# A two-layer diffusion backbone on one core: the order of every engine written out by the program, and the modulation spread over more stages

## The chip, the core and the metric

The kernel runs on one core of a Trainium2 chip. A core has five engines that run side by side and meet through semaphores: TensorE (matmuls; PE in the profile, PEld its weight loads), VectorE (DVE), ScalarE (ACT), GpSimd (POOL) and SyncE (SP), the last two used here mostly to issue DMAs. Each engine works off its own queue in order. The metric is the device time of one launch in microseconds (us).

## The reference, cut to what matters

Two layers over 256 latent tokens of width 1024, with 256 context tokens that only the first layer reads. Each layer is FFN half step, token mixing, FFN half step. Each sub-layer is wrapped in two RMS norms and a modulation that is computed from a conditioning vector:

```python
def pre(x, m, k, g):                       # shift and scale
    return rms_norm(x, g) * (1 + m[:, 3*k+1, None]) + m[:, 3*k, None]
def post(y, m, k, g):                      # gate
    return m[:, 3*k+2, None] * rms_norm(y, g)
def swiglu(h, w_gu, w_down):
    gt, up = jnp.split(h @ w_gu, 2, axis=-1)
    return (jax.nn.silu(gt) * up) @ w_down
m_lat = ada_mod(c, w_mod[i], b_mod[i])     # silu(c) @ w + b: nine vectors of 1024 per layer
x = x + 0.5 * post(swiglu(pre(x, m, 0, g[0]), ff1...), m, 0, g[1])
x = x + post(mixer(pre(x, m, 1, g[2])), m, 1, g[3])
x = x + 0.5 * post(swiglu(pre(x, m, 2, g[4]), ff2...), m, 2, g[5])
```

The first layer's mixer joins a depthwise convolution of 31 taps with a group norm (512 channels) and attention of 8 heads over a window with a bias plus all context keys. The second layer's mixer is a gated convolution of 3 taps. All inputs are float32.

## The kernel before, in words

**Weights.** All weight matrices lie in one flow of chunks of 16 tiles (128x128 each), in the order of use. `load` (L187) brings half a chunk (512 KB) on SP's queue; `piece` (L193) splits four tiles into a rounded part (`nc.scalar.copy`, L202) and a remainder (`nc.vector.tensor_sub`, L203). Every product is three matmuls (rounded x rounded, rounded x remainder, remainder x rounded): `mm3` (L213 to L217) with the weights stationary and 256 or 512 tokens moving, `rows3` (L286 to L291) with 128 tokens stationary and 512 output columns moving.

**Stages.** ff1_0 (latent and context, 512 tokens), ev_in, attention and convolution, ev_out, ff2_0, ff1_1, od_in, od_out, ff2_1. An FFN computes `gate_up` (silu on ScalarE, product on VectorE, split on both; L330 to L334) for each of 22 groups of 128 columns, then the down matmuls. In ff1_0 this goes in five parts of 4, 4, 4, 5 and 5 groups; the first three groups of part one are accumulated together (`grp`) while the inputs are being normalised, and after each part's groups its down matmuls run for four blocks of 128 tokens (L537 to L539). In the later FFNs the first three groups are computed token-major (`head`, L317), and `Out` (L295) runs the down matmuls for two token blocks: all but the last 6 rows of tiles for both blocks, then that tail (`TAIL`) for the first block and for the second.

**Norm steps.** `residual` (L246) squares the block, multiplies by the gate row, takes the power -1/2 on POOL (L240), updates x (L258) and repeats square and power for the next norm. `turn` (L265) scales the rows, transposes them on TensorE (L274), applies scale and shift per channel (L279) and splits (L283, L284).

**Modulation.** 128 tiles of `wmodb` (512 KB each) come on POOL's queue into four slots; `mod_dot` (L129) reduces one with the conditioning vector on VectorE, the first 24 tiles twice (latent and context). `bg(n)` does the next n dots: 4 after each group of ff1_0 and 2 after each down block (`BG0`), one per group in ff2_0 (`BG1`), the rest at ff2_0's end. `gate_row` (L169) writes the gate vector to DRAM and reads it back onto all partitions as a row, both on POOL's queue.

**Order.** The program emits instructions as its loops run; a planner then orders each engine's queue by its own estimates and priorities. `high_priority(offset=AHEAD)` moves the norm steps up. The convolution's taps (L599) are handed out between attention steps by fixed counts (`CONV_AT`); `scores` and `weigh` do one head pair and token block at a time.

Of the kernel before, what the change touches and what calls it, by code (L numbers as in the profile page):

```python
# [47 lines left out]
AHEAD = 300  # L48
MOD_PE = (0, 1, 2, 4, 6)
PARTS0 = (4, 4, 4, 5, 5)  # L50
BG0 = (4, 2)
BG1 = 1
CONV_AT = (2, 4, 6, 10, 8, 8)
CONV_ORDER = ((0, 0), (0, 1), (1, 0), (0, 2), (1, 1), (0, 3), (1, 2), (1, 3))
EV_ORDER = (6, 4, 5, 0, 1, 2, 3, 7)
EV_TAIL = 4
RING = 12
EXTRA = ("X2", "X3", "Y2", "Y3")
# [4 lines left out]
def hybrid_kernel(ctx: ExitStack, tc: tile.TileContext, xT, ctxT, xtok, crow, smalls, wmoda, wmodb, wflow, bias,  # L63
# [5 lines left out]
    wraw = ctx.enter_context(tc.tile_pool(name="wraw", bufs=5))  # L69
    whi = ctx.enter_context(tc.tile_pool(name="whi", bufs=RING))  # L70
    wlo = ctx.enter_context(tc.tile_pool(name="wlo", bufs=RING))
    mraw_p = ctx.enter_context(tc.tile_pool(name="mraw", bufs=4))
# [3 lines left out]
    ps_mm = ctx.enter_context(tc.tile_pool(name="ps_mm", bufs=6, space=bass.MemoryType.PSUM))  # L76
    ps_bc = ctx.enter_context(tc.tile_pool(name="ps_bc", bufs=2, space=bass.MemoryType.PSUM))

    def bank(pool, name):
        return pool.tile([P, 512], F32, name=name)  # L80
# [32 lines left out]
    for n in range(4):  # L113
        ps = bank(ps_mm, "mm")
        nc.tensor.matmul(ps, lhsT=ident[0:4, n:n + 1].to_broadcast([4, P]), rhs=crow_t, start=True, stop=True)
        nc.scalar.activation(cbf[:, n * 512:(n + 1) * 512], ps, AF.Silu)
# [11 lines left out]
    def mod_dot(row, l, v, ch, j):  # L128
        nc.vector.scalar_tensor_tensor(junk, row, 1.0, cb[:, v, :], op0=ALU.mult, op1=ALU.mult,  # L129
                                       accum_out=mraw[:, l, v, ch, j:j + 1])  # L130

    def mod_jobs():
        order = [(0, 2, (0, 1)), (0, 3, (0, 1)), (0, 4, (0, 1))]
        order += [(0, ch, (0,)) for ch in (5, 6, 7, 8)] + [(1, ch, (0,)) for ch in range(9)]
        n = 0
        for l, ch, conds in order:
            for j in range(KD):
                cur = mraw_p.tile([P, D], F32, name="mr", tag="mr")
                nc.gpsimd.dma_start(out=cur, in_=wmodb[n])  # L139
                for v in conds:  # L140
                    mod_dot(cur, l, v, ch, j)
                    yield
                n += 1

    jobs = mod_jobs()

    def bg(n):
        for _ in range(n):
            if next(jobs, 0) == 0:
                return  # L150


    def mod_pre(l, v, k):
# [3 lines left out]
        nc.vector.tensor_add(t, mraw[:, l, v, 3 * k + 1, :], bm[:, l, 3 * k + 1, :])  # L157
        nc.vector.scalar_tensor_tensor(a, t, 1.0, g[:, l, 2 * k, :], op0=ALU.add, op1=ALU.mult)
        nc.vector.tensor_add(b, mraw[:, l, v, 3 * k, :], bm[:, l, 3 * k, :])
        return a, b  # L160

    def mod_post(l, v, k, res):
        p = const.tile([P, KD], F32, name=f"p{l}{v}{k}")
        t = small.tile([P, KD], F32, name="mt")
        nc.vector.tensor_add(t, mraw[:, l, v, 3 * k + 2, :], bm[:, l, 3 * k + 2, :])
        nc.vector.scalar_tensor_tensor(p, t, res, g[:, l, 2 * k + 1, :], op0=ALU.mult, op1=ALU.mult)
        return p

    def gate_row(l, v, k, res):  # L169

        p = mod_post(l, v, k, res)
        flat = dram.tile([KD, P], F32, name=f"prow{l}{v}{k}")
        nc.gpsimd.dma_start(out=flat.rearrange("k p -> p k"), in_=p)
        row = mraw_p.tile([P, D], F32, name="pr", tag="mr")
        nc.gpsimd.dma_start(out=row, in_=flat.rearrange("k p -> (k p)").partition_broadcast(P))
        return row

# [9 lines left out]
    def load(n, m):  # L187
        if (n, m) not in raws:
            raws[n, m] = wraw.tile([P, RAW], F32, name="wr")
            nc.sync.dma_start(out=raws[n, m], in_=wflow[n][:, m * RAW:(m + 1) * RAW])  # L190
        return raws[n, m]

    def piece(n, q):  # L193
        if (n, q) not in chunks:
            r = load(n, q // 2)[:, (q % 2) * PIECE:(q % 2 + 1) * PIECE]
            if n >= offs["ff2_0"] + 3 and q == SPLIT - 1:
                both = page("wx", EXTRA[n % 4], [P, 2, PIECE], F32R)
                h, lo = both[:, 0, :], both[:, 1, :]
            else:
                h = whi.tile([P, PIECE], F32R, name="wh")  # L200
                lo = wlo.tile([P, PIECE], F32R, name="wl")
            nc.scalar.copy(h, r)  # L202
            nc.vector.tensor_sub(lo, r, h.bitcast(F32))  # L203
            chunks[n, q] = (h, lo)
        return chunks[n, q]

    def wtile(name, i, w=1):
        n, o = divmod(i, NTILE)
        q, o = divmod(o, NTILE // SPLIT)
        h, lo = piece(offs[name] + n, q)  # L210
        return h[:, o * P:(o + w) * P], lo[:, o * P:(o + w) * P]

    def mm3(ps, w, xh, xlo, start, stop, check=False):  # L213
        wh, wl = w
        nc.tensor.matmul(ps, lhsT=wh, rhs=xh, start=start, stop=False, skip_group_check=check)  # L215
        nc.tensor.matmul(ps, lhsT=wh, rhs=xlo, start=False, stop=False, skip_group_check=check)  # L216
        nc.tensor.matmul(ps, lhsT=wl, rhs=xh, start=False, stop=stop, skip_group_check=check)  # L217
# [10 lines left out]
    def spread(r, nt):  # L228
        bc = bank(ps_bc, "bc")
# [6 lines left out]
    def rstd(ss):  # L236
        u = small.tile([P, 1], F32, name="uu")
        nc.vector.scalar_tensor_tensor(u, ss[:, 0:1], EPS, ss[:, 1:2], op0=ALU.add, op1=ALU.add)  # L238
        r = small.tile([P, 1], F32, name="rr1")
        nc.gpsimd.tensor_tensor(r, u, nhalf[:, :1], op=ALU.pow)  # L240
        return r

    def square(ss, n, y):
        nc.scalar.activation(ajunk, y, AF.Square, scale=1.0 / 32, accum_out=ss[:, n:n + 1])

    def residual(y, row, x, yw, out_t=None):  # L246

        with tc.high_priority(offset=AHEAD):
            ss = small.tile([P, 2], F32, name="ss")
            for n in range(2):  # L250
                c = slice(n * 512, (n + 1) * 512)
                square(ss, n, y[n])
                nc.vector.tensor_mul(yw[:, c], y[n], row[:, c])
            r = rstd(ss)
            s2 = small.tile([P, 2], F32, name="s2")
            for n in range(2):
                c = slice(n * 512, (n + 1) * 512)
                nc.vector.scalar_tensor_tensor(x[:, c], yw[:, c], r, x[:, c], op0=ALU.mult, op1=ALU.add)  # L258
                if out_t is None:
                    square(s2, n, x[:, c])  # L260
                else:
                    nc.sync.dma_start(out=out_t[:, c], in_=x[:, c])
            return rstd(s2) if out_t is None else None

    def turn(x, rx, xs, a, b, h, t):  # L265

        ts = slice(t * P, (t + 1) * P)
        for n in range(4):
            c = slice(n * S, (n + 1) * S)
            with tc.high_priority(offset=AHEAD):  # L270
# [320 lines left out]
    def conv_ops():  # L591
        for part, i in CONV_ORDER:
# [9 lines left out]
            if part == 0:  # L602
                continue
# [308 lines left out]
```

## Time and profile before

| | before |
|---|---|
| median of 3 runs | 1310.84 us (1304.28 to 1314.84) |
| the profiled execution's own time | 1304.78 us |
| its span, first to last instruction | 1303.0 us |
| mean granted TensorE clock | 0.968 |
| HBM read | 255.55 MB |

The span is what the profile covers; the time of the same execution is 1.78 us more. "Busy" of TensorE contains modelled ends of pipelined matmuls, so a busy TensorE may still be slow; the count of matmuls in a stretch and the granted clock (1.00 is 2.4 GHz) tell more. "idle before" or "waited for" names what released an engine.

### The profile page before, as it was taken

The numbers are of one execution on the slowest core, as the hardware profiler recorded it, in microseconds if no ns is written. First come the engines' busy times: TensorE is split into PE (matmuls) and PEld (weight loads), VectorE is DVE, ScalarE is ACT, GpSimd is POOL, SyncE is SP. The second block draws the span as 40 slices with busy tenths as digits, with TensorE's granted clock in tenths as the row PEclk, the third lists the DMA queues.
The fourth block names the chain that finished last, engine by engine and source line by source line (L and its number), as shares of the span: only waits on it lengthen the run. The fifth ranks groups of instructions, "written<-read, shape, count | busy, mean of one in ns | idle before, by whom it ended". The sixth has DMA issues, their size and how long they took to land.

```text
span 1303.0 us, 19613 instructions
## 1 busy us (share of the span) xinstructions
PE 1216.9 (93%) x7206; PEld 1063.4 (82%) x7206; DVE 907.3 (70%) x1786; ACT 597.1 (46%) x1201; POOL 104.6 (8%) x180
## 2 busy tenths in 40 slices
PE   7999994995999999888999998999998998999997
PEld 4788883784888897667999986999986997999986
DVE  5999896977434999835899765766556776756652
ACT  5534221222233745546644455655545556555541
POOL 0111222222000100001011101000001001000000
PEclk9999997997999999988999998999998999999999
DMA  8968999998322341205799874555544544555540
GB/s 321 358 211 278 244 327 272 272 318 281 123 68 98 118 158 50 98 13 181 258 343 364 242 280 147 194 181 182 188 161 146 195 149 159 197 191 179 180 160 32
DMA packets 72776, 257.90 MB, mean 198 GB/s; under 512 B 8164, under 2 KB 10340, under 8 KB 72680
## 3 DMA queue, kind: packets, MB, share of 16 engines
q1 hardware_dynamic: 53016, 185.84, 42.1%
q0 software_dynamic: 19664, 70.82, 16.7%
q8 instruction: 56, 0.92, 0.3%
q14 instruction: 40, 0.33, 0.1%
HBM read 255.55 MB, written 1.08 MB: 197 GB/s over the span
## 4 chain that ended last, share of the span: by engine, by line
PE 71%; DVE 10%; DMA 8%; issue 5%; ACT 3%; POOL 2%; SPq 0%; DVEq 0%; POOLq 0%; ACTq 0%
PE mm L215 14%; PE mm L216 14%; PE mm L217 14%; PE mm L289 7%; PE mm L291 7%; PE mm L290 7%; DMA mr<-in_wmodb 7%; DVE bufD L599 3%; DVE junk L129 2%; PE mm L537 2%; PE mm L539 2%; PE mm L538 2%; DVE wl L203 2%; POOL rr L240 1%; DVE xt L258 1%
## 5 line engine op out<-in xcount | busy, mean ns | idle before, releaser
L202 ACT CAST wh<-wr 128x512 fp32r<-128x512 f32 x536 | 324.8, 620 | 327.7 <-PE mm L216 147.6
L203 DVE TENSOR_TENSOR wl<-wr,wh 128x512 fp32r<-128x512 f32 x536 | 359.3, 687 | 160.2 <-ACT wh L202 159.5
L215 PE MATMUL mm<-hin,wh 128*128 128x256 f32 x792 | 224.4, 283 | 0.0
L217 PE MATMUL mm<-hin,wl 128*128 128x256 f32 x792 | 224.1, 283 | 0.0
L216 PE MATMUL mm<-hin,wh 128*128 128x256 f32 x792 | 224.1, 283 | 0.0
L129 DVE SCALAR_TENSOR_TENSOR junk<-mr,cb 128x1024 bf16<-128x1024 f32 x156 | 190.1, 1218 | 45.6 <-DMA mr<-in_wmodb 45.2
L216 PEld LDWEIGHTS mm<-hin,wh 128*128 128x128 f32 x792 | 152.0, 192 | 0.0
L215 PEld LDWEIGHTS mm<-hin,wh 128*128 128x128 f32 x792 | 152.0, 192 | 0.0
L217 PEld LDWEIGHTS mm<-hin,wl 128*128 128x128 f32 x792 | 152.0, 192 | 0.0
L215 PE MATMUL mm<-hh,wh 128*128 128x512 f32 x352 | 137.3, 392 | 1.8 <-ACT hh L457 1.3
L216 PE MATMUL mm<-hl,wh 128*128 128x512 f32 x352 | 137.6, 391 | 0.0
L217 PE MATMUL mm<-hh,wl 128*128 128x512 f32 x352 | 137.4, 392 | 0.0
L537 PE MATMUL mm<-wh,Hh 128*128 128x512 f32 x176 | 70.8, 407 | 32.9 <-ACT Hh L333 32.9
L139 POOL DMA_DIRECT2D mr<-in_wmodb x128 | 68.2, 533 | 335.8 <-DVE junk L129 224.1
L203 DVE TENSOR_TENSOR wx<-wr,wx 128x512 fp32r<-128x512 f32 x112 | 77.0, 688 | 10.6 <-ACT wx L202 7.1
L215 PEld LDWEIGHTS mm<-hh,wh 128*128 128x128 f32 x352 | 66.3, 189 | 16.3 <-ACT hh L457 1.8
L217 PEld LDWEIGHTS mm<-hh,wl 128*128 128x128 f32 x352 | 66.7, 189 | 14.0
L216 PEld LDWEIGHTS mm<-hl,wh 128*128 128x128 f32 x352 | 66.4, 189 | 13.8
L240 POOL TENSOR_TENSOR rr<-uu,nhalf 128x1 f32<-128x1 f32 x26 | 19.8, 760 | 687.3 <-DVE uu L238 687.3
L215 PE MATMUL mm<-hin,wx 128*128 128x256 f32 x264 | 74.7, 283 | 0.0
L216 PE MATMUL mm<-hin,wx 128*128 128x256 f32 x264 | 74.7, 283 | 0.0
L217 PE MATMUL mm<-hin,wx 128*128 128x256 f32 x264 | 74.7, 283 | 0.0
(280 smaller groups left out, 2319.1 us busy)
## 6 DMA issues: line engine op xcount, KB each, us to landing
wr<-in_wflow SPq DMA_DIRECT2D x324, 512.0 KB, 5.1
mr<-in_wmodb POOLq DMA_DIRECT2D x128, 512.0 KB, 6.1
mr<-in_wmoda SPq DMA_DIRECT2D x8, 512.0 KB, 8.9
wme<-in_wmoda SPq DMA_DIRECT2D x8, 512.0 KB, 8.5
pr<-prow POOLq DMA_DIRECT2D x7, 512.0 KB, 7.2
xt<-in_xtok SPq DMA_DIRECT2D x4, 512.0 KB, 4.6
bt<-in_bias SPq DMA_DIRECT2D x4, 512.0 KB, 5.7
xlc<-in_xT SPq DMA_DIRECT2D x4, 256.0 KB, 4.5
```

The lines of the kernel that those rows point to most:

```text
L129: nc.vector.scalar_tensor_tensor(junk, row, 1.0, cb[:, v, :], op0=ALU.mult, op1=ALU.mult, accum_out=mraw[:, l, v, ch, j:j + 1])
L139: nc.gpsimd.dma_start(out=cur, in_=wmodb[n])
L202: nc.scalar.copy(h, r)
L203: nc.vector.tensor_sub(lo, r, h.bitcast(F32))
L215: nc.tensor.matmul(ps, lhsT=wh, rhs=xh, start=start, stop=False, skip_group_check=check)
L216: nc.tensor.matmul(ps, lhsT=wh, rhs=xlo, start=False, stop=False, skip_group_check=check)
L217: nc.tensor.matmul(ps, lhsT=wl, rhs=xh, start=False, stop=stop, skip_group_check=check)
L289: nc.tensor.matmul(ps, lhsT=src[:, 0, ts], rhs=wh, start=start, stop=False)
L290: nc.tensor.matmul(ps, lhsT=src[:, 0, ts], rhs=wl, start=False, stop=False)
L291: nc.tensor.matmul(ps, lhsT=src[:, 1, ts], rhs=wh, start=False, stop=stop)
L537: nc.tensor.matmul(y[n], lhsT=Hh0[:, k, ts], rhs=wh, start=k == 0, stop=False)
L599: nc.vector.scalar_tensor_tensor(acc[:, i, :], src, dwh[:, i, d:d + 1], acc[:, i, :], op0=ALU.mult, op1=ALU.add)
```

## The change

All instructions after the first three groups of ff1_0 go through a wrapper that pins each behind the one emitted before it on its engine. The program keeps three clocks (`clk`: TensorE, VectorE, ScalarE) that it advances by an estimate for each instruction, and uses them to decide where to emit steps of background tasks: generators that `spawn` starts and that `tick`, called by every `wtile`, resumes when TensorE's clock has reached the time that they yielded.

- Splits: 13 slots for pieces, rounded part and remainder in one page; `wtile` reads ahead by `LEAD` = 10 pieces in steady stretches (`auto`), `more` adds splits between norm steps.
- Norm steps: `Out.chain` holds one token block's steps; scale and shift are now rows (`pre_rows`, fetched through DRAM like the gate row) applied on VectorE before the transposes. In ff1_0, `chain0` does the same with scale and shift after the transposes, partly on ScalarE.
- The mixer: taps, group norms (`groups`) and attention (`unit`, two head pairs in flight) are tasks; the bias is negated on POOL, the scaling of the weights by 1/sum goes from ScalarE to POOL.
- Modulation: 72 tiles in ff1_0 (3 dots per group in part one, then 5), 21 each in ff2_0 and ff1_1, 6 in od_in, 8 in ff2_1.
- PSUM: eight banks handed out by `take` and `give`; the tail's tiles are stored in the order of use.

The core of the diff; lines left out are marked:

```diff
+            def call(*a, **kw):
+                ins = f(*a, **kw)
+                if pin[0]:
+                    tc.keep_in_program_order(ins)
+                    if self.cost:
+                        self.cost(nm, a, kw)
+                return ins
...
+    def tick():
+        while tasks:
+            due = [x for x in tasks if x[0] <= clk["pe"]]
+            if not due:
+                break
+            x = min(due, key=lambda x: x[0])
+            r = next(x[2], None)
...
+        while filler[0] and filler[0]():
+            pass
...
     def bg(n):
         for _ in range(n):
-            if next(jobs, 0) == 0:
+            if not mods["here"]:
                 return
+            cur, l, ch, conds, j = mods["here"][0]
+            mod_dot(cur, l, conds.pop(0), ch, j)
+            if not conds:
+                mods["here"].pop(0)
+                mod_load()
...
+    def to_row(p, name, slot):
+        flat = dram.tile([KD, P], F32, name=f"row{name}")
+        PO.dma_start(out=flat.rearrange("k p -> p k"), in_=p)
+        row = page("pr", slot)
+        PO.dma_start(out=row, in_=flat.rearrange("k p -> (k p)").partition_broadcast(P))
         return row
+    def pre_rows(l, k, slots):
+        return [to_row(p, f"{nm}{l}{k}", slot) for p, nm, slot in zip(mod_pre(l, 0, k), "ab", slots)]
...
     def wtile(name, i, w=1):
+        p, o = divmod(offs[name] * NTILE + i, NTILE // SPLIT)
+        f = feedst
+        f["at"] = p
+        feed(p + max(1, f["auto"]))
+        tick()
...
+        def chain(self, t):
+            y, yw, x, ss = self.y[t], self.yw[t], xt[t], small.tile([P, 2], F32, name="ss")
+            for n in range(2):
+                square(ss, n, y[n])
+                clk["dv"] = both()
+                DV.tensor_mul(yw[:, half(n)], y[n], self.row[:, half(n)])
+                give(y[n])
+                yield both() + 0.1
+            r = rstd(ss)
+            yield clk["dv"] + POW
+            s2 = update(yw, r, x, self.out_t and self.out_t[t])
+            if self.out_t is not None:
+                return
+            a, b = self.pre()
+            for n in range(2):
+                DV.tensor_mul(yw[:, half(n)], x[:, half(n)], a[:, half(n)])
+            yield both() + 0.1
+            r = rstd(s2)
+            yield clk["dv"] + POW
+            for c0, c1 in ((0, 2), (2, 4), (4, 8)):
+                c = slice(c0 * P, c1 * P)
+                DV.scalar_tensor_tensor(yw[:, c], yw[:, c], r, b[:, c], op0=ALU.mult, op1=ALU.add)
...
+    def steady():
+        filler[0] = None
+        feedst["auto"] = LEAD
...
+            bg(1 if f not in (5, 10) else 2)
+        bg(100)
+        row = gate_row(l, 0, k, 0.5, "M0")
+        rows = pre and pre_rows(*pre, ("Y2", "Y3"))
+        return Out(name, NF * 16, H, NF, TAIL, row, lambda: rows, out_t)
...
+    pin[0] = True
+    steady()
+    mod_begin(24 + 32 + 16, ("M0", "M1", "M2", "M3"))
...
         for f in range(nf):
             if pi == 0 and f < 3:
                 pg, pu = grp[f]
...
             gate_up(Hh0[:, f, :], Hl0[:, f, :], pg, pu, 512)
-            bg(BG0[0])
+            give(pg, pu)
+            bg(5 if pi else 3)
         base += nf * 16
         if last:
-            prow = [gate_row(0, v, 0, 0.5) for v in range(2)]
+            bg(100)
+            prow = [gate_row(0, v, 0, 0.5, f"M{v}") for v in range(2)]
...
+    def bias_load(i):
+        bts[i] = page("bt", f"M{2 + i % 2}", [P, 2, 2, S])
+        PO.dma_start(out=bts[i], in_=bias[i])
+        PO.tensor_scalar(bts[i], bts[i], -1.0, None, op0=ALU.mult)
...
+    def ev_rows():
+        if not ev_pre:
+            ev_pre.extend(pre_rows(0, 2, ("M2", "M3")))
+        return ev_pre
+    post = Out("ev_out", 0, src, KD, EV_TAIL, ev_row, ev_rows, None, mixer_fill)
...
+    od_row = gate_row(1, 0, 1, 1.0, "M0")
+    od_pre = pre_rows(1, 2, ("Y2", "Y3"))
+    post = Out("od_out", 0, mx, KD, TAIL, od_row, lambda: od_pre)
```

## Rows read from the trace of the kernel before

**Rows 1.** The page, parts 1 and 5: busy times; then line, engine, form, busy, mean ns

```profile
PE 1216.9 (93%) x7206; PEld 1063.4 (82%) x7206; DVE 907.3 (70%) x1786; ACT 597.1 (46%) x1201; POOL 104.6 (8%) x180
...
L202 ACT CAST wh<-wr 128x512 fp32r<-128x512 f32 x536 | 324.8, 620 | 327.7 <-PE mm L216 147.6
L203 DVE TENSOR_TENSOR wl<-wr,wh 128x512 fp32r<-128x512 f32 x536 | 359.3, 687 | 160.2 <-ACT wh L202 159.5
```

**Rows 2.** Windows: length, busy and count by engine, granted clock, DMA share, GB/s

```profile
134.00:200.00 66.00, 66.00 (x291) 54.34 (x290) 57.31 (x110) 17.33 (x30) 16.57 (x29) 1.00 0.93 284
200.00:260.00 60.00, 41.03 (x167) 32.45 (x167) 46.30 (x83) 10.52 (x18) 13.60 (x25) 0.83 0.93 274
260.00:330.00 70.00, 54.58 (x227) 43.82 (x226) 48.69 (x88) 14.70 (x27) 14.13 (x26) 0.88 0.90 302
...
1055.00:1060.00 5.00, 5.00 (x44) 5.00 (x44) 3.46 (x7) 2.23 (x5) 0.00 (x0) 1.00 0.55 189
```

**Rows 3.** Waits: who waited for whom: us in total, times, longest

```profile
DVE junk L129 <- DMA mr<-in_wmodb: 45.2, 31, 6.0
...
PE mm L537 <- ACT Hh L333: 32.9, 4, 11.1
...
PE bc L274 <- DVE xn L279: 13.8, 10, 4.8
```

**Rows 4.** Windows of 5 us around one long gap in the first FFN

```profile
225.00:230.00 5.00, 0.00 (x0) 0.00 (x0) 3.69 (x7) 0.24 (x1) 1.59 (x3) 0.50 0.98 363
230.00:235.00 5.00, 4.57 (x13) 3.69 (x14) 3.90 (x7) 0.37 (x1) 1.06 (x2) 0.62 0.84 275
```

**Rows 5.** Timeline of VectorE: start, us, line, form, idle before it and releaser

```profile
27.98 1.22 DVE L129 SCALAR_TENSOR_TENSOR junk<-wme,cb 128x1024 bf16<-128x1024 f32 x1
...
29.24 1.23 DVE L129 SCALAR_TENSOR_TENSOR junk<-wme,cb 128x1024 bf16<-128x1024 f32 x1
...
62.75 0.69 DVE L332 TENSOR_TENSOR gh<-gs,mm 128x512 f32<-128x512 f32 x1 [0.71 <-PE mm L217]
```

**Rows 6.** DMA issues at 75 to 134, 260 to 330, 850 to 930: median us to landing

```profile
mr<-in_wmodb POOLq DMA_DIRECT2D x16, 512.0 KB, 4.9
...
mr<-in_wmodb POOLq DMA_DIRECT2D x22, 512.0 KB, 6.5
...
wr<-in_wflow SPq DMA_DIRECT2D x28, 512.0 KB, 3.7
```

**Rows 7.** DMA issues of the whole span

```profile
bt<-in_bias SPq DMA_DIRECT2D x4, 512.0 KB, 5.7
...
sm_in<-in_small SPq DMA_DIRECT2D x1, 208.0 KB, 2.4
```

**Rows 8.** Timeline of POOL: two row writes, and the reads that wait for them

```profile
732.66 1.81 POOL L173 DMA_DIRECT2D prow<-p  x2 [6.12 <-DVE mt L165]
742.21 0.56 POOL L175 DMA_DIRECT2D pr<-prow  x1 [7.73 <-DMA prow<-p]
747.06 0.55 POOL L175 DMA_DIRECT2D pr<-prow  x1 [4.29 <-DMA prow<-p]
```

**Rows 9.** The tile of the broadcast row: landing of its reads

```profile
DMA to landing us min/median/max: 5.3/7.2/10.3
```

**Rows 10.** Windows: the last part of the mixer before ev_out

```profile
550.00:578.70 28.70, 21.44 (x114) 14.15 (x113) 10.96 (x44) 13.64 (x35) 2.01 (x2) 0.88 0.00 1
```

**Rows 11.** Windows: the changes into ff2_0, ff1_1 and ff2_1

```profile
601.40:629.00 27.60, 23.18 (x115) 18.58 (x114) 20.95 (x50) 18.78 (x44) 3.67 (x5) 0.88 0.41 135
798.70:826.80 28.10, 22.69 (x114) 18.36 (x113) 20.07 (x47) 17.89 (x41) 1.18 (x3) 0.88 0.37 122
1098.50:1124.30 25.80, 21.78 (x114) 17.64 (x113) 20.02 (x47) 17.97 (x41) 1.22 (x3) 0.93 0.40 134
```

**Rows 12.** Timeline around the change into ff1_1: ScalarE's first step, TensorE's transposes

```profile
791.36 0.60 ACT L244 ACTIVATE ajunk<-mm 128x512 bf16<-128x512 f32 x1 [3.50 <-PE mm L291]
...
799.39 0.84 PE L274 MATMUL bc<-ident,yw 128*128 128x128 f32 x4
```

More of the change, by code (lines that the diff above doesn't have):

```diff
@@ L75, in hybrid_kernel, with cols @@
     small = ctx.enter_context(tc.tile_pool(name="small", bufs=4))
[L76 to L80, printed above, removed]
+    psum = ctx.enter_context(tc.tile_pool(name="psum", bufs=1, space=bass.MemoryType.PSUM))
+    pin = [False]
+    clk = {"pe": 0.0, "dv": 0.0, "ac": 0.0}
+    def cols(ap):
+        n = 1
+        for v in ap.shape[1:]:
+            n *= v
+        return n
@@ new lines, in need, with bank @@
+    def need(cond):
+        for _ in range(5000):
+            if cond():
+                return
+            clk["pe"] = max(clk["pe"], min(x[0] for x in tasks))
+            tick()
+        raise AssertionError("a task that waits for what never comes")
+    rot = {}
+    def bank(kind):
+        n = rot.get(kind, 0)
+        rot[kind] = n + 1
+        tag = f"P{n % 6}" if kind == "mm" else f"P{6 + n % 2}"
+        return psum.tile([P, 512], F32, name=kind, tag=tag)
+    free = [f"P{n}" for n in (6, 7)]
@@ L83, in hybrid_kernel, with take, give @@
+    held = {}
+    def take(name="mm"):
+        need(lambda: free)
+        tag = free.pop(0)
+        ps = psum.tile([P, 512], F32, name=name, tag=tag)
+        held[id(ps)] = (tag, ps)
+        return ps
+    def give(*ps):
+        for b in ps:
+            free.append(held.pop(id(b))[0])
     sm_in = const.tile([P, 416], F32, name="sm_in")
@@ L185, in hybrid_kernel @@
     raws = {}
[L187 to L205, printed above, removed]
@@ L207, in wtile, with load @@
-    def wtile(name, i, w=1):
[L208 to L211, printed above, removed]
+    PIECES = total * SPLIT
+    slots = [f"R{n}" for n in range(RING)]
+    casts = {}
+    feedst = {"done": 0, "cast": 0, "at": 0, "hold": None, "auto": 0}
+    def load(m):
+        if m < 2 * total and m not in raws:
+            raws[m] = wraw.tile([P, RAW], F32, name="wr")
+            SY.dma_start(out=raws[m], in_=wflow[m // 2][:, m % 2 * RAW:(m % 2 + 1) * RAW])
@@ L246, in residual @@
[L246 to L263, printed above, removed]
@@ new lines, in hybrid_kernel, with update @@
+    half = lambda n: slice(n * 512, (n + 1) * 512)
+    def update(yw, r, x, out_t=None):
+        s2 = small.tile([P, 2], F32, name="s2")
+        for n in range(2):
+            DV.scalar_tensor_tensor(x[:, half(n)], yw[:, half(n)], r, x[:, half(n)], op0=ALU.mult, op1=ALU.add)
+            if out_t is None:
+                clk["ac"] = both()
+                square(s2, n, x[:, half(n)])
+            else:
+                SY.dma_start(out=out_t[:, half(n)], in_=x[:, half(n)])
+        return s2
@@ L408, in load_mod @@
         else:
-            wm[j] = [mraw_p.tile([P, D], F32, name="mr", tag="mr") for _ in range(2)]
+            wm[j] = [page("mr", f"M{j % 2 * 2 + u}") for u in range(2)]
         for u in range(2):
@@ L669, in keys @@
+        give(ps)
+        st_["v"] = t + 1
+    need(turned)
+    mixer_pages()
+    ev_row = gate_row(0, 0, 1, 1.0, "M0")
+    bias_load(0)
+    for n in range(2 * CT):
+        spawn(unit(n))
+    for i in range(CT):
+        ps = take()
         for k in range(KD):
```

801 lines of the change are left out of this document (486 added, 315 removed).

## The prediction

> **What bounds the kernel now.** I read the busy times first, then the windows by stage, then who waited for whom, then single stretches. TensorE is called busy for 1216.9 of 1303.0 us, VectorE 907.3, ScalarE 597.1 [rows 1], so only TensorE's gaps and slow stretches can be won. In a stretch without gaps 291 matmuls fill 66 us, 0.227 us for one of 512 columns; 44 of 256 columns fill 5 us, 0.114 each [rows 2]. The windows show where that rate fails first: from 200 to 260 us 167 matmuls (37.9 us) and from 260 to 330 us 227 (51.5 us), 40.6 us lost, at a granted clock of 0.83 and 0.88 [rows 2]. The waits name the cause: the down matmuls of line 537 sat 32.9 us in four waits for the gate product [rows 3]. VectorE was not slow there, it was in the wrong order: modulation dots stood ahead of the gate product and waited 45.2 us for their tiles [rows 3]. Elsewhere 13.8 us go to line 274, behind line 279, at the stage changes [rows 3].
>
> TensorE's clock adds to each long gap: it read 0.50 (1.2 GHz) through the 5 us before matmuls resumed at 230.4, 0.62 in the next 5 [rows 4]. So some 4 us of work run at half rate after a long stall: I add 2 us to each.
>
> **The change, part by part.** Everything after the first three gate groups is pinned to the order in which the program emits it. I follow that order by hand, with durations of the old trace.
>
> (a) *Entry to the pinned order.* The three groups end at E. The program then emits gate_up, three dots, gate_up, three dots, gate_up, three dots, and only then the splits for the fourth group, because the read-ahead of ten pieces begins with that group's first wtile. A dot repeats every 1.26 us (27.98 to 29.24) [rows 5]; a gate product holds VectorE 0.61 us, waits for ScalarE's cast (0.62) and subtracts in 0.61, 1.95 with the handovers [rows 1, 5]. Today the first product starts at 62.75, 0.7 us after its bank [rows 5]; 12 matmuls (2.7 us) follow that bank, so E is 64.7 and the first pair ends at E. Then 9 dots (11.3) and two pairs (3.9) end at E+15.2, and one split of 0.69 [rows 1] makes the weights ready: 15.8 us of empty TensorE. Now the planner has put those splits ahead and nothing is lost. **+17.8** with the clock.
>
> (b) *The first FFN's modulation.* The 40.6 us go as they are: gate_up now precedes its dots. What is late next is the fifth dot. There are four tile slots; slot one is refilled after dot one. Landing takes 4.9 us at moderate load and 6.5 in the worst stretch [rows 6], so dot five is ready 1.26+0.1+0.54+4.9 = 6.8 us after the first starts, where it could run at 5.0: 1.8 us lost, 3.4 at worst. VectorE's load per group is 5 dots (6.3), 4 splits (2.4) and the pair (1.95), 10.65 of TensorE's 10.9, so the loss is not made good before the part ends. Parts one to three run mostly double dots (48 on 24 tiles) and lose only the last pair's latency, some 0.8 us each; in part four the lag grows over four groups to 4x(1.8-0.2) = 6.4 us, and 2 of clock; in part five over three, less 1.5 for a group of four dots, 3.3. Together 14. **-26.6** (bounds -14 and -37).
>
> (c) *Gate rows at the end of the first FFN.* Each is a write of 4 KB to DRAM and a broadcast read, both on POOL's queue, the read waiting for the write. Today the planner issues them far ahead; pinned, they stand behind the last group. D is the start of the last down phase (27 us); the write leaves at D+3. Bounds for a write: as quick as the fastest small load, 2.4 us [rows 7], or as slow as today's, 9.5 (732.66 to 742.21) [rows 8]; for a read 3.7, a weight piece in a quiet stretch [rows 6], to 7.2, the median [rows 9]. The second of two writes landed 4.9 us after the first [rows 8], which with a fixed 2 us makes 6.9 for one alone; I take 6.5, and 5.3 (the shortest) for the read [rows 9]. Row one lands at D+15; the multiply on VectorE waits for it from D+7.5, with additions and splits queued behind. Then two powers, the update and the scaling: first transposes near D+23. TensorE reaches them at about D+15, since the program places them without knowing of the row: 8+2, less today's 1.8 in that place. **+8**.
>
> (d) *Mixer.* In its last 28.7 us VectorE works only 11 and TensorE runs at 0.88 [rows 10]: the attention units and group norms run one behind another there. Units in pairs and norms between key matmuls attack that tail. From below: VectorE's idle 17.7 us all go, -18. From above: POOL now negates each bias after its load (5.7 us [rows 7]) ahead of the unit's scaling in its queue, three times up to 7 us: +12 with half the tail won. I take **-7**, half of the tail less 2.
>
> (e) *Mixer to second FFN.* ev_rows fetches both rows inside the chain of the first token block, after update. From the end of its matmuls, T: square, power and update take 4.1 us, half of the chain of 8.2 that runs from 791.2 to the transposes at 799.39 today [rows 12]. Write a leaves at T+4.7, lands at 11.2, its row at 16.5; write b leaves at 11.8, lands at 18.3, its row at 23.7. POOL's in-order queue also holds the second power until 18.9. Then addition, transposes, cast: T+25.2. The cover is the second block's tail, 24 matmuls, 5.4 us. Stall 19.8, clock 2, less today's 6.7 (counted as in (f)): **+15**.
>
> (f) *The two changes into and out of ff1_1.* Rows are fetched under 43 us of down matmuls: free. If that cover went, (e) is the price. Today 4.8 us are lost at the transposes, since VectorE holds the next pair behind other work [rows 3]; the stretch of 28.1 us has 16.4 of head matmuls and 4.5 of transposes, 7.2 over, and by the same count 27.6 and 25.8 us leave 6.7 at ev_out's end and 4.9 at od_out's [rows 11]. The pinned order removes the gap. It trades eight scalings per block for two multiplies and three additions, about even; but twelve splits and both chains are some 20 us of VectorE (20.07 busy there now [rows 11]) in the 17 us to the end of the first head, so 3 to 4 us stay. **-6** for two.
>
> (g) *od_out into ff2_1.* Three row trips in POOL's queue start 4.9 us after od_in ends (S); only 21.8 us of matmuls follow. The third read is issued at S+26, and the power of the first block stands behind it: chain through at S+33. Stall 11, clock 2, less 4.9: **+8**.
>
> Dots in ff2_0 and ff1_1 cost nothing: one of 1.26 us for each group of 5.5, in which VectorE is busy 3.46 of 5 us [rows 2]; without that idle time all 42 would cost 53. Prologue and last chain stay.
>
> Sum: 17.8-26.6+8-7+15-6+8 = **+9.2**. The profiled execution took 1304.78 us (span 1303.0), so 1314; the median of the runs shown is 6.1 above that one, so I forecast **1320 us**, a rise of 0.7%, inside the 1% (1298 to 1324) that can't be told from no change.
>
> **Rivals.** *Short trips, faster.* If a write lands in 2.4 us and a row in 3.7 [rows 6, 7], (c) becomes -1, (e) +5.6 and (g) -4, and with a mixer at -15 the sum is -29: about 1282. For it: those phases carry little DMA. Against it: neither of the writes that the trace times took under 9.5 us [rows 8]. The Trainium skill, DMA: Bandwidth & Descriptors, "Anatomy of one DMA", gives a transfer a fixed 2.0 us and its bytes at 436 GB/s, as an estimate 2.0 us for the write and 3.2 for the read; by that this rival holds, but no trip in this trace was that quick.
>
> *Slow trips, slower.* Its place is POOL's queue in (c), (e) and (g): with 9.5 and 7.2 us [rows 8, 9] the second row of (e) lands at T+31.7, which makes (e) +23, (c) +14 and (g) +19, and dots at 6.5 us landing make (b) -14. Sum +47: about 1358. It decides once a trip exceeds some 13 us. For it: the times are those measured; against: they were measured beside busy transfers.
>
> *Order alone does little.* The pin binds issue order only; where the planner's order was nearly that already, gains and losses shrink together, about 1311. Against it: dots and rows stand in another order today.
>
> **Numbers.** Forecast 0.52 (1308 to 1334: half of it within 1%, half over); short trips 0.28; slow trips 0.15; little effect 0.05. So faster 0.27, same 0.32, slower 0.41. The range 1276 to 1348 leaves out about a tenth on each side.
>
> **What would show it.** (a) one gap of about 16 us before the fourth gate group, with nine dots in it. (b) waits of line 537's successor gone in parts one to three, two of 3 to 7 us left. (c), (e), (g) a write and a read on POOL with TensorE empty behind them; under 5 us each, the short rival is right. (d) a mixer 7 us shorter. (f) no gap at the transposes and a clock of 1.00. I am wrong if the splits of group four run ahead of the dots, or if the mixer shrinks by over 20 us.

## The result, and the profile after

The changed kernel takes **1456.4 us** (median of 4 runs, 1455.7 to 1466.4) against 1309.3 for the kernel before on the same chip: a ratio of **1.114** (95% interval 1.107 to 1.121), slower. The forecast of 1320 and its range both missed, and so did the slow rival's 1358. The profiled execution has a span of 1453.9 us, 150.9 more than before; the mean granted clock is 0.924 in place of 0.968.

The page first, then the waits. All pinned instructions carry the wrapper's line, L109, so one goes by tiles.

```profile
PE 1231.8 (85%) x7222; PEld 1069.9 (74%) x7222; DVE 907.4 (62%) x1708; ACT 570.2 (39%) x1169; POOL 140.3 (10%) x220
...
PE 28%; issue 26%; DMA 26%; DVE 11%; ACT 5%; POOL 2%; SPq 0%; POOLq 0%; DVEq 0%; ACTq 0%
...
L109 DVE TENSOR_TENSOR wx<-wr,wx 128x512 fp32r<-128x512 f32 x648 | 411.1, 686 | 154.8 <-ACT wx L109 154.1
L109 ACT CAST wx<-wr 128x512 fp32r<-128x512 f32 x648 | 367.5, 618 | 334.6 <-DMA wr<-in_wflow 281.3
```

```profile
ACT wx L109 <- DMA wr<-in_wflow: 281.3, 123, 14.0
...
POOL pr L109 <- DMA rowp<-p: 79.9, 7, 13.4
PE bc L109 <- DVE yw L109: 75.6, 4, 33.7
...
POOL pr L109 <- DMA rowa<-a: 52.7, 4, 14.6
...
POOL pr L109 <- DMA rowb<-b: 47.1, 4, 14.1
...
PE mm L109 <- DVE bufD L109: 22.3, 2, 12.5
...
PE mm L109 <- POOL rv L109: 21.2, 3, 18.3
```

The arithmetic is what it was (VectorE 907.3 in [rows 1], 907.4 here; a split still takes 0.62 and 0.69 us). The waits are new: the 32.9 us that TensorE waited for the gate product in [rows 3] have shrunk to 2.8, with 4.5 more for a weight split in the same place. Instead it sits before transposes (75.6 us in four waits, one of 33.7), POOL waits 179.7 us for its own row writes, and ScalarE's casts wait 281.3 us for weights (60.0 in the kernel before). The windows (columns as in [rows 2]) show five of the new holes and one slow stretch:

```profile
411.50:428.50 17.00, 0.00 (x0) 0.00 (x0) 5.21 (x10) 3.29 (x9) 1.67 (x3) 0.65 0.36 109
522.00:545.00 23.00, 4.69 (x33) 4.16 (x32) 4.29 (x11) 1.67 (x5) 6.04 (x6) 0.66 0.23 61
612.00:634.00 22.00, 4.38 (x18) 2.52 (x16) 18.23 (x41) 1.43 (x3) 1.20 (x1) 0.63 0.09 32
667.00:700.00 33.00, 0.32 (x2) 0.29 (x2) 5.75 (x15) 3.67 (x9) 4.11 (x6) 0.53 0.29 66
833.40:904.80 71.40, 63.91 (x267) 50.17 (x265) 34.98 (x62) 28.01 (x53) 4.91 (x7) 0.98 0.87 190
1219.00:1253.00 34.00, 0.54 (x2) 0.29 (x2) 11.98 (x23) 9.76 (x23) 4.08 (x6) 0.54 0.54 137
```

The first is the wait for a gate row at the end of ff1_0; the second and third lie in the mixer; the fourth and sixth are the changes into ff2_0 and ff2_1, 33 and 34 us with TensorE empty. The fifth is ff2_0's down matmuls, where the DMA engines are busy 0.87 of the time and move only 190 GB/s. The same 267 matmuls before:

```profile
739.30:799.50 60.20, 60.20 (x267) 49.48 (x266) 32.31 (x54) 29.36 (x57) 3.45 (x4) 1.00 0.67 221
```

From TensorE's first and last matmuls of each kind, stage by stage, in us, one profiled execution of each kernel; the four right columns are experiments below.

| stage | before | after | rows in 32 bytes | + splits, mixer unpinned | unpinned, 32 bytes | before, dots pinned |
|---|---|---|---|---|---|---|
| start to first down matmul | 76.1 | 96.1 | 93.6 | 77.8 | 75.4 | 76.0 |
| to the last down matmul of ff1_0 | 358.4 | 346.0 | 331.9 | 351.7 | 329.6 | 320.8 |
| mixer and ev_out | 167.8 | 224.9 | 217.1 | 161.1 | 165.2 | 167.5 |
| change into ff2_0 | 5.3 | 36.2 | 17.2 | 12.5 | 9.6 | 5.3 |
| ff2_0 down | 60.2 | 71.4 | 60.2 | 60.2 | 66.1 | 60.2 |
| ff1_1 down | 60.2 | 71.1 | 60.2 | 60.2 | 60.2 | 60.2 |
| od_out to ff2_1 | 4.6 | 37.2 | 12.2 | 13.3 | 4.1 | 4.6 |

The remaining stages agree within 5 us in all columns. The trips behind the fourth window, in POOL's timeline (columns as in [rows 8]), and the landing times of all of them (columns as in [rows 7]):

```profile
668.81 0.99 POOL L109 DMA_DIRECT2D rowa<-a  x1 [3.53 <-DVE b L109]
679.62 0.56 POOL L109 DMA_DIRECT2D pr<-rowa  x1 [9.82 <-DMA rowa<-a]
681.97 0.92 POOL L109 DMA_DIRECT2D rowb<-b  x1 [1.79 <-issue]
692.78 0.55 POOL L109 DMA_DIRECT2D pr<-rowb  x1 [9.89 <-DMA rowb<-b]
693.35 1.09 POOL L109 TENSOR_TENSOR rr<-uu,nhalf 128x1 f32<-128x1 f32 x2
```

```profile
pr<-rowp POOLq DMA_DIRECT2D x7, 512.0 KB, 6.8
...
pr<-rowa POOLq DMA_DIRECT2D x4, 512.0 KB, 7.5
pr<-rowb POOLq DMA_DIRECT2D x4, 512.0 KB, 6.5
...
rowp<-p POOLq DMA_DIRECT2D x7, 4.0 KB, 12.0
rowa<-a POOLq DMA_DIRECT2D x4, 4.0 KB, 14.6
rowb<-b POOLq DMA_DIRECT2D x4, 4.0 KB, 12.0
```

Two writes of some 10 us one behind the other, even in a stretch with little other DMA (0.29), and the power of the second block behind both.

### The profile page after: what moved, and what is told of

It reads as the page before. It is cut to its first block, busy times and chain, and to the rows that moved or that the text cites. A ratio compares the mean times of both kernels' runs of the same rounds, so it can differ in the third digit from the quotient of the medians.

```text
span 1453.9 us, 19337 instructions
## 1 busy us (share of the span) xinstructions
PE 1231.8 (85%) x7222; PEld 1069.9 (74%) x7222; DVE 907.4 (62%) x1708; ACT 570.2 (39%) x1169; POOL 140.3 (10%) x220
## 4 chain that ended last, share of the span: by engine, by line
PE 28%; issue 26%; DMA 26%; DVE 11%; ACT 5%; POOL 2%; SPq 0%; POOLq 0%; DVEq 0%; ACTq 0%
PE mm L109 26%; DMA wr<-in_wflow 15%; DVE wx L109 4%; DMA mr<-in_wmodb 4%; DMA rowp<-p 3%; DVE bufD L109 3%; PE bc L109 2%; DMA rowa<-a 2%; DVE junk L109 2%; ACT wx L109 1%; ACT ajunk L109 1%; POOL mr L109 1%; DMA rowb<-b 1%; ACT xn L109 1%; DVE yw L109 1%
## 5 line engine op out<-in xcount | busy, mean ns | idle before, releaser
L109 DVE TENSOR_TENSOR wx<-wr,wx 128x512 fp32r<-128x512 f32 x648 | 411.1, 686 | 154.8 <-ACT wx L109 154.1
L109 ACT CAST wx<-wr 128x512 fp32r<-128x512 f32 x648 | 367.5, 618 | 334.6 <-DMA wr<-in_wflow 281.3
L109 PE MATMUL mm<-hin,wx 128*128 128x256 f32 x3168 | 381.7, 283 | 0.0
L109 PEld LDWEIGHTS mm<-hin,wx 128*128 128x128 f32 x3168 | 380.6, 192 | 0.0
L109 PE MATMUL mm<-hh,wx 128*128 128x512 f32 x704 | 224.1, 398 | 14.8 <-ACT wx L109 11.0
L109 DVE SCALAR_TENSOR_TENSOR junk<-mr,cb 128x1024 bf16<-128x1024 f32 x156 | 190.7, 1222 | 12.5 <-DMA mr<-in_wmodb 10.1
L109 PEld LDWEIGHTS mm<-hh,wx 128*128 128x128 f32 x704 | 134.9, 192 | 45.4 <-ACT wx L109 11.6
L109 PE MATMUL mm<-hl,wx 128*128 128x512 f32 x352 | 139.3, 396 | 0.0
L109 POOL DMA_DIRECT2D mr<-in_wmodb x128 | 67.9, 531 | 621.1 <-DVE junk L109 592.3
L109 PE MATMUL mm<-wx,Hh 128*128 128x512 f32 x352 | 112.0, 400 | 7.2 <-DVE wx L109 4.5
L109 DVE TENSOR_TENSOR gh<-gs,mm 128x256 f32<-128x256 f32 (+2 forms) x93 | 43.7, 474 | 78.3 <-PE mm L109 39.1
L109 PE MATMUL mm<-wx,hin 128*128 128x256 f32 (+1 forms) x384 | 78.9, 360 | 12.8 <-ACT hin L109 12.8
L109 PEld LDWEIGHTS mm<-wx,Hh 128*128 128x128 f32 x352 | 67.6, 193 | 22.0 <-DVE wx L109 4.9
L109 PE MATMUL mm<-wx,Hb 128*128 128x512 f32 x288 | 72.0, 401 | 8.7 <-ACT wx L109 7.8
L109 PEld LDWEIGHTS mm<-wx,hin 128*128 128x128 f32 x384 | 61.7, 199 | 23.1 <-ACT hin L109 15.1
L109 PEld LDWEIGHTS mm<-hl,wx 128*128 128x128 f32 x352 | 67.7, 192 | 14.0
L109 PE MATMUL bc<-ident,yw 128*128 128x128 f32 x64 | 13.9, 329 | 75.6 <-DVE yw L109 75.6
L109 PEld LDWEIGHTS mm<-wx,Hb 128*128 128x128 f32 x288 | 54.4, 191 | 24.4 <-ACT wx L109 10.3
L109 PE MATMUL mm<-wx,Hl 128*128 128x512 f32 x176 | 70.2, 399 | 0.0
L109 PE MATMUL mm<-hla,wx 128*128 128x256 f32 x384 | 60.7, 304 | 10.8 <-ACT hla L109 9.9
L109 PEld LDWEIGHTS bc<-ident,yw 128*128 128x128 f32 x64 | 10.0, 173 | 80.3 <-DVE yw L109 44.2
L109 ACT ACTIVATE gs<-mm 128x256 f32<-128x256 f32 (+2 forms) x91 | 38.3, 425 | 68.0 <-PE mm L109 67.9
```

The source lines that it names most:

```text
L109: ins = f(*a, **kw)
```

## The experiments

Theory A held that two things cost the time: the trips of rows through DRAM, and engines that wait in a fixed order. Each ratio is against the kernel before on the same chip, with its 95% interval.

**Rows made on the chip.** Eight small matmuls and two copies replace each of the fifteen trips (seven gate rows, four pairs of scale and shift).

```diff
-        PO.dma_start(out=flat.rearrange("k p -> p k"), in_=p)
...
-        PO.dma_start(out=row, in_=flat.rearrange("k p -> (k p)").partition_broadcast(P))
...
+                PE.matmul(ps[:, q * P:(q + 1) * P], lhsT=p[:, 4 * n + q:4 * n + q + 1].to_broadcast([P, P]),
+                          rhs=ident, start=True, stop=True)
...
+                AC.copy(row[:, half(n)], ps)
```

> The changed kernel, with each of its 11 rows made by eight small matmuls and two copies on the core instead of a write to DRAM and a read back; nothing else differs. Theory A, the trips: in the changed kernel the two long gaps before the transposes (32.8 and 33.7 us), the 17.0 us gap at the end of the first FFN, the 18.3 us gap in the mixer (a power queued behind a row's trip and the bias on POOL) and some 11 us in each of the down phases of ff2_0 and ff1_1 (weights that arrive late while rows are written) all hang on the trips: 1456 falls by 90 to 115 us, to 1340 to 1365, and the down phases return from 70 to 60 us. Rival B, the pinned order by itself: the norm steps on VectorE are what those stretches wait for and the trips only lie beside them: under 40 us, above 1415.

1375.3 us, 1.049 (1.047 to 1.050): 81 less than the changed kernel, short of theory A's 90 to 115, since the matmuls that make the rows now stand on TensorE (48 of them, 5.6 us, in each of the down phases of ff2_0 and ff1_1, which took 66 and 67 us). The changes into ff2_0 and ff2_1 fell to 6.9 and 7.1 us. The mixer with ev_out stayed at 214.

**Splits first at the entry.** `feed(12 + LEAD)` ahead of the first gate product.

> The changed kernel, with the splits of the ten pieces of the fourth gate group emitted before the first three gate products and their nine dots. Theory A: the gap of 10.6 us before the fourth group and the one of 3.3 us in it go, with 2 us of clock: 1456 becomes about 1441 (1438 to 1446). Rival: the weights arrive late anyhow, and the dots are then late by as much: no more than 4 us gained.

1446.5, 1.103 (1.100 to 1.106): 10 less, at the upper edge of theory A. The entry went from 96.1 to 79.3 us; 3.8 and 5.8 us came back as gaps at the next down matmuls.

**The kernel before with only its dots pinned.**

```diff
-                    mod_dot(cur, l, v, ch, j)
+                    tc.keep_in_program_order(mod_dot(cur, l, v, ch, j))
```

> The kernel before, with one edit: each modulation dot is pinned behind what the program emitted before it on VectorE, so the planner can no longer put dots ahead of the gate product; tiles, counts and all else stay. Theory A: the stalls of the down matmuls in the first FFN came from that order alone: 25 to 38 us faster than before, 1272 to 1284. Rival, bandwidth: the tiles arrive too late whatever stands first, and the dots of a part then delay its last gate product all the same: within 8 us of before.

**1269.1, 0.968** (0.965 to 0.971), faster than both kernels and 3 us better than theory A's span. The stretch that [rows 2] showed at 167 and 227 matmuls is full:

```profile
200.00:260.00 60.00, 60.00 (x266) 49.68 (x265) 49.90 (x87) 17.56 (x29) 13.00 (x24) 1.00 0.91 296
260.00:330.00 70.00, 70.00 (x311) 57.98 (x310) 55.42 (x95) 20.67 (x34) 12.84 (x25) 1.00 0.79 275
```

So the reading of the bottleneck was right, and one pinned kind of instruction is enough to remove it.

**Taps ahead of VectorE's clock.** `clk["dv"] < clk["pe"] + 12` in place of 1.2 for taps.

> The changed kernel, with the convolution's taps allowed to run 12 us ahead on the program's VectorE clock instead of 1.2. Theory A: VectorE stands idle in the mixer behind waits of the attention steps while 60 taps are left for the end, where TensorE waits 12.5 and 9.8 us for them; with the taps earlier these two gaps go and the mixer shortens by 15 to 25 us: 1431 to 1441. Rival: the taps then stand ahead of the norm and attention steps in VectorE's queue and delay those by as much: within 6 us of 1456 or above it.

1438.7, 1.096 (1.093 to 1.099): 18 less, within theory A. After the last key matmul 8 taps were left in place of 60, and TensorE's two waits for them were gone; but it now waited 22.8 us for splits, and the mixer with ev_out still took 210 us (224.9 in the changed kernel). So taking the left-over taps away in this manner is worth some 15 us there, and the rival is right about a part.

**Taps at a fixed rate,** 1.3 for each us of TensorE's clock, on top of rows made on the chip; and the same with splits first:

> The changed kernel with its rows made on the chip, and the convolution's taps handed out at 1.3 for each us of the program's TensorE clock, whatever its VectorE clock says. Theory A (VectorE sits behind waits while taps are held back; 61 of 124 taps of 0.485 us are left when the last key matmul is through, against 3 in the kernel before): the mixer falls from 214 us to 180-195 and the median from 1375 to 1340-1358; fewer than 25 taps are left at the end of the key matmuls. Rival (the taps only trade places with splits and norm steps on a full VectorE): 1370 or more, with new waits of TensorE for splits.

> The same, and the ten pieces' splits put ahead of the gate products and dots at the entry to the pinned order. If the three costs (rows 81, entry 10, taps 20-30) are separate places and add: 1330-1348, still over the kernel before by 1.5 to 3 per cent, what is left being the chains of norm steps, the matmuls that make the rows, and the rest of the mixer. If they overlap: over 1355. Under 1312 would say that the pinned order itself costs nothing.

1353.1, 1.030 (1.026 to 1.034), and 1348.8, 1.028 (1.025 to 1.031): 22 and 27 less than with the rows alone. The mixer with ev_out fell from 214 to 195, the upper edge of what was expected; 32 taps were still left after the last key matmul, more than the 25 allowed. (The count of 3 for the kernel before was taken some us after its last key matmul; at that matmul it was 11.) Splits first added 4 and not 10: the entry gained 22, of which 14 came back in ff1_0 (332.5 to 346.1) and 9 in the down phases of ff2_0 and ff1_1.

What the taps tell, by VectorE's groups up to the last key matmul and after it, in the kernel before:

```profile
L599 DVE SCALAR_TENSOR_TENSOR bufD<-av,dwh,bufD 128x256 f32<-128x256 f32 x110 | 47.4, 475 | 0.0
...
L599 DVE SCALAR_TENSOR_TENSOR bufD<-av,dwh,bufD 128x256 f32<-128x256 f32 x11 | 5.3, 479 | 0.1
```

and in the changed kernel:

```profile
L109 DVE SCALAR_TENSOR_TENSOR bufD<-av,dwh,bufD 128x256 f32<-128x256 f32 x60 | 29.1, 484 | 1.7
...
L109 DVE SCALAR_TENSOR_TENSOR bufD<-av,dwh,bufD 128x256 f32<-128x256 f32 x60 | 29.1, 484 | 1.9
```

Half of them, 29 us of VectorE, are left for a time when TensorE has little else to do than wait for them.

**No pins, same emission order.** `tc.keep_in_program_order` is not called; the program's clocks run on.

> The changed kernel with the same emission order and the same clocks, but no instruction pinned: the planner orders each queue, as in the kernel before. Theory A (what costs is mostly the trips through DRAM in the chains and in-order waits): the entry gap and the left-over taps go (-35 to -50), the trips stay in data dependence, so 1390-1430. Rival (the pin itself is the cost, since a planner would have put the trips ahead too): 1310-1340. Second rival (the emission order is what the planner needs help with): 1456 or more.

1333.3, 1.016 (1.014 to 1.019): 123 less, inside the rival's span and far from theory A's. The trips left the chains: the changes into ff2_0 and ff2_1 fell to 6.8 and 2.2 us. But ff2_0's down phase took 100.9 us, and its trace holds the clearest view of a row write. First POOL, then weights (landing in 700 to 845 us), then the phase as a whole:

```profile
742.03 0.93 POOL L109 DMA_DIRECT2D rowb<-b  x1 [1.58 <-DVE b L109]
742.96 0.90 POOL L109 DMA_DIRECT2D rowp<-p  x1
743.84 0.88 POOL L109 DMA_DIRECT2D rowa<-a  x1
```

```profile
DMA to landing us min/median/max: 4.2/7.2/22.4
```

```profile
743.70:844.60 100.90, 69.93 (x266) 54.23 (x264) 50.47 (x93) 29.90 (x61) 11.61 (x18) 0.81 0.82 183
```

Three writes of 4 KB in a row (and three more at 778), and a weight load lands after 22.4 us; TensorE, waiting for weights, stood for 13.5 us up to 771 and for 12.6 up to 802. The DMA engines are busy 0.82 of this phase and move 183 GB/s.

**Rows in pieces of 32 bytes.** The changed kernel, pinned, with the write alone altered (the read still takes the 4 KB as they lie in DRAM; the channels come in another order, so the values are not the reference's):

```diff
-        flat = dram.tile([KD, P], F32, name=f"row{name}")
-        PO.dma_start(out=flat.rearrange("k p -> p k"), in_=p)
+        flat = dram.tile([P, KD], F32, name=f"row{name}")
+        PO.dma_start(out=flat, in_=p)
...
-        PO.dma_start(out=row, in_=flat.rearrange("k p -> (k p)").partition_broadcast(P))
+        PO.dma_start(out=row, in_=flat.rearrange("p k -> (p k)").partition_broadcast(P))
```

> The changed kernel with each row's 4 KB written as it lies in SBUF, 128 pieces of 32 bytes in place of 1024 of 4 bytes (leaves the channels of each row in another order, so the values are not the reference's). Theory A (the write's many small elements make the trip long, and hold up the weight loads beside it): a write lands in 3-5 us in place of 9-14.6, the gaps of 33 us shrink to some 18, the median falls by 45-70 to 1386-1411. Rival (the time is that of the queue or of a write's completion, whatever its pieces): writes still over 8 us and under 20 us gained.

**1365.9, 1.041** (1.038 to 1.044): 91 less, more than theory A's 70. The writes (issues, then the waits for them):

```profile
rowp<-p POOLq DMA_DIRECT2D x7, 4.0 KB, 2.6
rowa<-a POOLq DMA_DIRECT2D x4, 4.0 KB, 7.4
rowb<-b POOLq DMA_DIRECT2D x4, 4.0 KB, 4.9
```

```profile
POOL pr L109 <- DMA rowa<-a: 24.8, 4, 8.2
POOL pr L109 <- DMA rowb<-b: 18.7, 4, 5.6
POOL pr L109 <- DMA rowp<-p: 17.8, 7, 6.2
```

and the down phase of ff2_0, to be held against 71.4 us above:

```profile
791.00:851.30 60.30, 60.25 (x266) 49.41 (x264) 37.91 (x66) 30.60 (x59) 4.08 (x7) 1.00 0.68 232
```

The same bytes from the same queue at nearly the same places: the trip shortens and the weights beside it are on time. What made both was the 1024 pieces of 4 bytes.

The trace's list of DMA packets shows both effects. A write is 16 packets of 256 bytes in either form. The fifteen writes of the changed kernel landed 5.5 to 11.7 us after the last of their packets had ended, those in 32-byte pieces less than 0.9 us after. Packets of 4 KB, in which weights and other loads come, take 0.16 us by their median; 194 of them took over 2 us in the changed kernel, the longest 7.8, and 6 with 32-byte pieces, the longest 2.6.

**Unpinned with rows in 32 bytes** (VectorE takes the row through a strided view, so the values are the reference's), and the same with only the dots pinned:

> The changed kernel unpinned (1333), with each row written as 128 pieces of 32 bytes and read back in that order by a strided view, so that the values are the reference's. Theory A (a write of 1024 pieces of 4 bytes holds up the weight loads beside it: in the unpinned run three such writes at 742 to 745 us were followed by gaps of 13.5 and 12.6 us while TensorE waited for weights): those gaps go, and the median falls by 22-38 to 1295-1311. Rival (the gaps came from modulation tiles that are all fetched at once there): both gaps stay over 8 us and the median is over 1322.

> The same, with only the modulation dots pinned behind what is emitted before them. If the order of the dots is the part of the written-out order that wins (gaps of 6.4, 8.2, 6.6 and 8.7 us at down matmuls in the unpinned run, as in the kernel before): 25-35 less than the run without that pin, 1262-1285. Rival (something else delays the gate products): within 10 of it.

1286.2, 0.983 (0.979 to 0.986), and **1270.2, 0.970** (0.967 to 0.972). The first beat its span: 47 less than unpinned with 4-byte pieces. The second gained 16, between its theory (25 to 35) and its rival (10): only one stall of the four was left at the down matmuls of ff1_0 (7.3 us), and another 6 us came from ff2_0's down phase. It equals the kernel before with pinned dots, so the other parts of the change, without pins and with short row writes, gain nothing beyond the dots.

**The kernel before, dots pinned, rows in 32 bytes.**

> The kernel before with pinned dots (1269) and with its gate rows written in 32-byte pieces. Its seven rows are fetched ahead of need, so only the weight loads beside them can gain: 1258-1268. Rival (no weight is late there): the same within 4.

1274.5, 0.974 (0.970 to 0.977): no gain over 0.968, as the rival said, though 5 us more (on another chip, and the intervals overlap) and not within its 4; of these, 4 stand ahead of the first down matmul, where no row is used. Its rows are few and fetched early.

**Pinned, with three cures:** 32-byte rows, splits first, taps at a rate.

> The changed kernel, every engine pinned, with three cures together: rows written in 32-byte pieces, splits first at the entry, taps at a fixed rate. If the places are separate the sum is 1456-90-10-22 = 1334 (1324-1342), still 1 to 2.5 per cent over the kernel before; what is left then stands in the chains between stages (some 3+3 us at each change), the ends of ff1_0 and the mixer's power behind a row trip. Under 1312 would say that nothing is wrong with the pin itself; over 1348 that the cures overlap.

1353.3, 1.033 (1.031 to 1.036): a miss by 19. The cures do not add: against short writes alone (1365.9) splits first gained some 2 us by the end of ff1_0 and the taps 16 in the mixer. With ev_out it still took 200.6 us, with 10.2 us of waiting for a group norm's power behind a row trip and the negated bias in POOL's queue.

**Unpinned in the mixer alone,** with 32-byte rows and splits first: all engines, VectorE alone, and VectorE, ScalarE and POOL.

```diff
-                    tc.keep_in_program_order(ins)
+                    if self.eng not in loose:
+                        tc.keep_in_program_order(ins)
```

> The changed kernel with rows in 32-byte pieces and the splits first at the entry (some 1356 by the sum of those two), and no pin from the first instruction of the mixer's input products to the last that ev_out emits; every other stage stays pinned. Theory A (the pin within the mixer is the cost): mixer and ev_out take 165-178 us in place of 201 to 217, the median 1296-1320. Rival (what the pinned chains leave at its two ends decides): over 195 us there, and over 1336.

> The same, but in the mixer VectorE alone is unpinned. If VectorE's waits in fixed order, with taps behind them, are the cost: 165-185 us and 1296-1325, near the run with all engines unpinned. Rival (TensorE's fixed places for scores, transposes and group-norm products wait for results that the planner would have put later): over 195 us, over 1336.

> The same with VectorE, ScalarE and GpSimd unpinned in the mixer and TensorE and the loads pinned. By theory A within 8 us of the run with all unpinned; by the rival (TensorE's order) within 8 us of the one with VectorE alone, and both over 195 us in the mixer.

1313.3, 1.001 (1.000 to 1.003); 1328.8, 1.013 (1.010 to 1.016); 1333.4, 1.015 (1.012 to 1.018). The mixer with ev_out took 161, 176 and 183 us; the second run's median is 4 us over its span. Up to the last key matmul VectorE does 266 instructions in 105.6 us in the kernel before, 263 in 112.7 with the whole mixer unpinned, and 199 in 142.5 in the changed kernel (in this order):

```profile
434.50:540.10 105.60, 100.59 (x696) 89.65 (x695) 100.16 (x266) 57.40 (x126) 3.21 (x4) 0.98 0.36 120
```

```profile
429.60:542.30 112.70, 105.06 (x733) 92.59 (x732) 106.67 (x263) 66.50 (x154) 19.21 (x22) 0.98 0.37 119
```

```profile
442.00:584.50 142.50, 110.93 (x738) 97.17 (x737) 82.37 (x199) 67.23 (x151) 27.11 (x26) 0.88 0.30 94
```

So the pin within the mixer is the cost (217.1 us with short writes, 161 without the pin), and VectorE's fixed order is most of it (176); the other engines' fixed places are worth the last 15 us. That split depends on the order in which engines are freed. The third run is 20 us from the first, against theory A, and within 8 of the second, as its rival had it, but with a mixer well under the rival's 195 us: freeing ScalarE and POOL as well made the mixer 7 us longer than VectorE alone, and why stays open; from there, freeing TensorE and the loads is worth 22.

## Why the prediction was wrong

The sum was +9.2; the spans differ by 150.9. By its steps, with the stage table:

- **(a) Entry, +17.8: right.** +20.0. VectorE's timeline has the nine dots and two pairs between 66.9 and 81.9 us, and TensorE's gaps are 10.6 and 3.3 us; splits first took them away.
- **(b) Modulation in ff1_0, -26.6: right.** Where [rows 3] had 32.9 us, two waits of 2.8 (for the gate product) and 4.5 us (for a weight split) are left, both at part four's down matmuls, where 6.4 was forecast; the 3.3 of part five did not come.
- **(c) Gate rows at the end of ff1_0, +8: right place, half the size.** A gap of 17.0 us up to 428.5; with rows in 32 bytes it is 2.5. (b) and (c) together came to -12.4 where the sum had -18.6.
- **(d) Mixer, -7: the wrong sign, +57.** This is the largest miss. I saw idle VectorE at the mixer's end [rows 10] and credited the new tasks with filling it. I did not follow VectorE's queue through the pinned mixer: a tap is emitted only while the program's VectorE clock is less than 1.2 us ahead of TensorE's, what is emitted between taps then waits in order (up to the last key matmul VectorE stood 10.7 us before reductions of the scores, 10.7 before the splits of the context and 18.5 before the first group norm), and the idle time of that wait cannot be used by the taps behind it. 60 of 120 were left in place of 11. Unpinning the mixer gave 161 us, VectorE alone 176. The taps are a part only: with 8 left the mixer still took 210. For the bound of +12 I had only POOL's work in mind; its queue did hold the power for 18.3 us, behind a row trip that the bound left out.
- **(e) and (g), +15 and +8: right mechanism, half and a quarter of the size.** +31 and +33. The order of steps on POOL was the one forecast; a write took 12.0 to 14.6 us and a read 6.5 to 7.5 (medians), not 6.5 and 5.3. The step that failed is "which with a fixed 2 us makes 6.9 for one alone": it took the second write's 4.9 us after the first as the price of a write, and no run shows a fixed part of 2 us in a 4-byte write. Two writes in flight at once can land close together however long each takes: in [rows 8] the second was issued 0.9 us after the first, and its read left at 747.06, 13.5 us later. The list of issues of the kernel before has 10.5 us for its writes (a landing is recorded for one of the seven). In (e) the two writes took 10.5 us each, which is 8 of the 16 us that the forecast lacked. The rest of the chain was priced too low as well: with 32-byte pieces (writes of 2.4 and 3.8 us) the change into ff2_0 still took 17.2 us, 11.9 over the kernel before, where the short rival had +5.6. By the measured trips the slow rival was right in kind. It came to 1358 and not 1456 mainly because it kept (d) and (f).
- **(f) Changes around ff1_1, -6, "free": wrong, +26.** The rows had cover, as said. They were not free for what covered them: down phases of 71.4 and 71.1 us for 60.2, TensorE waiting for weights; with 32-byte pieces both are back at 60.2. I treated a write of 4 KB as nothing on the DMA engines because of its bytes. The changes themselves grew by 2 us each.
- **Dots in ff2_0 and ff1_1 at no cost: right.** Gate stages of 130.4 and 131.4 us against 131.8 and 130.9.

(a) to (g) measured: 20.0 - 12.4 + 57.1 + 30.9 + 26.3 + 32.6 = 154.5; the other stages gave back 3.6. Counted by runs instead of steps, short row writes take 91 us off the changed kernel, and an unpinned mixer with splits first 53 more (1313). Those 53 lie in the mixer (217.1 to 161.1): with short writes, splits first only moved a wait, since ff1_0 ended at 425.5 us without it and at 429.5 with it. The costs overlap: taking off the pins alone gave 123 and short writes alone 91, both together 170. The result with the mixer unpinned is the kernel before, within 1%, and what pinned dots would have won (43 us) is still spent: at the pinned changes of stage (12.5 us into ff2_0 and 13.3 into ff2_1, against 5.3 and 4.6) and in ff1_0 (352 us against 321).

The Trainium skill, DMA: Bandwidth & Descriptors, "Anatomy of one DMA", gives a fixed 2.0 us plus the time of the bytes, an estimate of 2.0 us for this write. The 32-byte form agrees where nothing stands ahead of it (1.7 to 2.7 us); the 4-byte form (9.4 us at the least in the changed kernel) does not. The same page, "Why small descriptors are slow", says that each descriptor has a fixed overhead on top of its bytes; the runs agree in direction, and show that neighbouring transfers pay too.

## What to carry to other kernels

Price a transfer by its pieces and not its bytes, and look for who shares the DMA engines with it: a vector written out 4 bytes at a time held up half-megabyte loads, and laying it out in 32-byte pieces was worth 91 us where chains waited for it. In the kernel before, whose rows are fetched early, it gained nothing. Pin the one kind of instruction that the trace shows out of place (here a line, worth 3%) before pinning an engine: a fixed order turns every wait of one instruction into a wait of all behind it. When a task is handed out against a program's own clock, count in the trace how much of it is left when its cover ends.

## What the runs showed of the hardware

- A write of 4 KB as 1024 pieces of 4 bytes landed in 12.0 to 14.6 us (medians), as 128 pieces of 32 bytes in 2.6 to 7.4, the longer ones behind a read of 512 KB in the same queue.
- Such a write landed 5.5 to 11.7 us after its last packet had ended, the 32-byte form less than 0.9 us after.
- Beside writes in 4-byte pieces a weight load of 512 KB in ff2_0's down phase took up to 24.3 us (pinned) and 22.4 (unpinned); with 32-byte pieces none took over 8.1 and 7.1.
- In holes of 33 and 34 us the granted clock read 0.53 and 0.54 (1.2 GHz).
- POOL's negation of a tile of 128x1024 took 2.77 us.
